# Moving the modulation sums of a two-layer backbone's up products from VectorE, ScalarE and GpSimd to TensorE

## The chip, the cores and the metric

The kernel runs on one core of one Trainium2 chip. TensorE, VectorE, ScalarE, GpSimd and SyncE are the core's engines; rows of the profile call them PE (and PEld for its weight loads), DVE, ACT, POOL and SP. The metric is the device time of one execution in microseconds (us), lower is better.

## The reference, cut to what matters

Two layers of a diffusion backbone work on 512 latent and 256 context tokens of 1024 features, all in fp32. Layer 0 mixes tokens by attention, layer 1 by a state-space layer; each is followed by a gated feed-forward with 2816 hidden features. Every sub-layer is steered by *modulations*: rows of 1024 numbers (shift, scale, gate) that come from a condition vector.

```python
silu_c = jax.nn.silu(c)          # latents' condition, 1024 numbers
silu_cc = jax.nn.silu(c_ctx)     # contexts' condition
for i in range(DEPTH):
    m_l = [... for m in jnp.split(silu_c @ w_mod[i] + b_mod[i], N_MOD, axis=-1)]
    m_c = jnp.split(silu_cc @ w_mod[i] + b_mod[i], N_MOD, axis=-1)
    ...
    h_l = modulate(rms_norm(x_lat, g_pre_ffn[i]), m_l[3], m_l[4])
    x_lat = x_lat + m_l[5] * rms_norm(conv_ffn(h_l, w_up[i], conv_w[i], conv_b[i], w_down[i]), g_post_ffn[i])
```

One modulation is a vector of 1024 times a matrix of 1024 x 1024, that is 4 MB of weights for a million multiplications: it is used once and is small work on much data. The feed-forward's first product, `h @ w_up` (768 or 512 tokens by 1024 by 5632), is the large one. It is called the up product here.

## The kernel before, in words

`ffn_up` computes the up products feature-major, in 22 *blocks* of 128 value and 128 gate features. For a block two chunks of `w_up` (128 x 1024, 512 KB) are loaded by SP into one of five slots (tag `raw`), and each is split into two fp32r parts, the rounded one by ScalarE (line 110) and the rest by VectorE (line 111). Three fp32r products then stand for one fp32 product (`mm3`, lines 147 to 149). In layer 0 each product runs over 512 latent columns (`b512`) and 256 context columns (`b256`), in layer 1 over the latents alone. The sums, two of them a block, lie in pairs of PSUM banks (tag `big`, three of them). ScalarE (872, 903) and VectorE (876 twice, 904) turn them into hidden features by the convolution and the gate; only then is the pair of banks free again.

While layer 0's up products run, two more things are done in jobs between the blocks:

- *Matrices of the state-space layer.* VectorE (1242, 1244) and GpSimd (1243) multiply tables (`PT`, later `QT`); TensorE transposes or multiplies them (`pP`, line 1261; `pK`, line 1290) into one of the two remaining PSUM banks (tag `aux`), ScalarE and VectorE take them out (1262, 1293 to 1298).
- *Later modulations.* `UP_MODS` names six units (layer, group, half): two with both conditions and three with the latents' alone in layer 0's up products, one in layer 1's. A unit takes eight chunks of `w_mod` (128 inputs x 1024 outputs, 512 KB) from the same five slots, in the same order as the chunks of `w_up`; two chunks go with a block in layer 0 from block 2 on, one with each of the blocks 8 to 15 in layer 1. `mods_ahead` (269) sums a chunk with the condition's number as a scale for each partition: for one condition VectorE alone (301) or ScalarE (295) followed by an addition on GpSimd (297). At the end of a unit TensorE adds up the partitions by a product with ones (308), and VectorE adds the bias and applies the gain (309 to 313).

Who does what next is decided when the program is built: instructions are put in order on each engine by a planner that simulates the program, and each engine then works through its own queue in that order. The order therefore shifts with any change of the code.

Of the kernel before, what the change touches and what calls it, by code (L numbers as in the profile page):

```python
# [19 lines left out]
P = 128  # L20
# [113 lines left out]
class Kernel:  # L134
# [78 lines left out]
    def mods_rows(self, l, grp):  # L213
        """The bias, and the gain of the norm that the two modulations of a group go with, as rows."""
# [17 lines left out]
    def mods_end(self, l, grp, acc, bg, psum, tag="aux", bufs=2, ms=(0, 1)):  # L232
        """Evacuates a group, stores its rows and, where they are wanted, turns them into columns."""
# [38 lines left out]
    def mods_ahead(self, psum, pool, units, lcs):  # L272
        """Modulations by other engines than the tensor engine, whose sums over partitions alone it takes; as jobs,
        one for each chunk of the weights."""
        nc, v, I = self.nc, self.nc.vector, self.I
        ones = pool.tile([P, 32], FT, name="ones")
        nc.gpsimd.memset(ones, 1.0)
        n = 64 * lcs
        for l, grp, m in units:
            b = self.small.tile([P, 512], FT, name="mbias", tag="mbias", bufs=1)[:n]  # L280
            g = self.small.tile([P, 512], FT, name="mgain", tag="mgain", bufs=1)[:n]
            name = {(0, 1): "g_pre_mix", (1, 0): "g_post_mix", (2, 0): "g_pre_ffn", (2, 1): "g_post_ffn"}.get((grp, m))
            for lc in range(lcs):
                c = slice(64 * lc, 64 * lc + 64)
                nc.sync.dma_start(b[c], dap(I["b_mod"], l * 6144 + grp * 2048 + m * D, [[512, 2], [0, 32], [1, 512]]))
                if name:
                    nc.sync.dma_start(g[c], dap(I[name], l * D, [[512, 2], [0, 32], [1, 512]]))
# [17 lines left out]
            for lc in range(lcs):  # L305
# [10 lines left out]
            for lc in range(lcs):  # L316
                nc.gpsimd.dma_start(dap(self.mdram[l, grp], lc * 2048 + m * D, [[512, 2], [1, 512]]),
                                    b[64 * lc:64 * lc + 64:32, :])
            if l and (grp, m) in ((1, 1), (2, 0)):
                p = psum.tile([P, 4, P], FT, name="pmc", tag="aux", bufs=2)  # L320
                for i in range(4):
                    nc.tensor.transpose(p[:, i, :64], b[:, i * P:(i + 1) * P], self.ident[:64, :64])
                v.tensor_copy(self.cols[1, 1][:, 0, grp - 1, :].rearrange("p (q b) -> p q b", b=4),
                              p[:, :, 0:33:32].rearrange("p b q -> p q b"))
# [35 lines left out]
    def stats(self, x, junk, tag):  # L360
        """x: rows, in one piece or in two; junk: room for their squares."""
# [14 lines left out]
    def plan_proj(self, w, nblk):  # L376
        """w: rows of inputs by columns; in blocks of 512 columns, two blocks of 128 rows a chunk."""
# [1441 lines left out]
```

## Time and profile before

| | us |
|---|---|
| median of 3 runs (lowest, highest) | 1744.71 (1743.69, 1745.6) |
| profiled execution, first to last instruction | 1744.2 |
| layer 0's up products, 421 to 922 us of it | 501 |
| layer 1's up products, 1365 to 1615 us of it | 250 |

The profile has no other time of its execution than this span; it lies 0.5 us under the median. In the rows below a busy time is the union of an engine's instructions. Matmuls are pipelined, so that each is shown longer than the step from its start to the next one's. "PEclk" is the mean clock that TensorE was granted, as a share of 2.4 GHz, its upper level; the lower one is 1.2 GHz. An engine that "waits" stands with its next instruction at the head of its queue, and all that is queued behind it waits too.

### The profile page before, as it was taken

The numbers are of one execution on the slowest core, as the hardware profiler recorded it, in microseconds if no ns is written. First come the engines' busy times: TensorE is split into PE (matmuls) and PEld (weight loads), VectorE is DVE, ScalarE is ACT, GpSimd is POOL, SyncE is SP. The second block draws the span as 40 slices with busy tenths as digits, with TensorE's granted clock in tenths as the row PEclk, the third lists the DMA queues.
The fourth block names the chain that finished last, engine by engine and source line by source line (L and its number), as shares of the span: only waits on it lengthen the run. The fifth ranks groups of instructions, "written<-read, shape, count | busy, mean of one in ns | idle before, by whom it ended". The sixth has DMA issues, their size and how long they took to land.

```text
span 1744.2 us, 22858 instructions
## 1 busy us (share of the span) xinstructions
PE 1552.6 (89%) x8376; PEld 1247.0 (71%) x8376; DVE 1166.4 (67%) x2036; ACT 772.0 (44%) x1470; POOL 373.3 (21%) x251
## 2 busy tenths in 40 slices
PE   6998489999988888998899999873789999999997
PEld 3775358888867776777788877542568888888886
DVE  4654377768999987888773357689934756565334
ACT  3564256756534333333332245555453534443322
POOL 0111060000255524334410011347501001100000
PEclk8999699999999899999999999886799999999999
DMA  9425181167354546465654269665252424432421
GB/s 308 139 73 170 37 244 47 45 225 256 116 149 136 168 135 198 126 177 179 188 144 163 97 197 273 191 170 183 91 190 85 133 85 145 134 96 97 169 73 48
DMA packets 225445, 256.39 MB, mean 147 GB/s; under 512 B 20621, under 2 KB 176917, under 8 KB 225077
## 3 DMA queue, kind: packets, MB, share of 16 engines
q1 hardware_dynamic: 224900, 254.85, 47.2%
q8 instruction: 66, 1.08, 0.3%
q14 instruction: 47, 0.38, 0.1%
q0 software_dynamic: 384, 0.07, 0.0%
q10 hardware_dynamic: 48, 0.01, 0.0%
HBM read 216.95 MB, written 34.80 MB: 144 GB/s over the span
## 4 chain that ended last, share of the span: by engine, by line
PE 58%; DVE 21%; DMA 8%; issue 5%; ACT 4%; SPq 3%; POOL 2%; DVEq 0%; ACTq 0%; POOLq 0%
PE up L147 6%; PE up L148 6%; PE up L149 6%; PE dn L148 5%; PE dn L147 5%; PE dn L149 5%; DVE whl L111 3%; PE acc L147 2%; DMA wraw<-in_w_mod 2%; PE acc L149 2%; PE acc L148 2%; DVE PT L1242 2%; PE glu L147 2%; PE glu L149 1%; PE glu L148 1%
## 5 line engine op out<-in xcount | busy, mean ns | idle before, releaser
L111 DVE TENSOR_TENSOR whl<-wraw,whl 128x1024 fp32r<-128x1024 f32 x202 | 277.0, 1376 | 176.8 <-ACT whl L110 169.0
L110 ACT ACTIVATE whl<-wraw 128x1024 fp32r<-128x1024 f32 x206 | 216.9, 1056 | 194.8 <-PE dn L149 128.2
L147 PE MATMUL up<-b,whl 128*128 128x256 f32 (+1 forms) x728 | 251.9, 349 | 23.2 <-DVE h L876 18.5
L148 PE MATMUL up<-b,whl 128*128 128x256 f32 (+1 forms) x728 | 249.9, 345 | 0.1
L149 PE MATMUL up<-b,whl 128*128 128x256 f32 (+1 forms) x728 | 249.0, 345 | 0.0
L147 PEld LDWEIGHTS up<-b,whl 128*128 128x128 f32 x728 | 144.0, 199 | 49.1 <-issue 22.6
L148 PE MATMUL dn<-whl,hs 128*128 128x512 f32 x440 | 172.9, 395 | 3.2 <-DVE whl L111 3.1
L149 PE MATMUL dn<-whl,hs 128*128 128x512 f32 x440 | 172.1, 394 | 0.0
L147 PE MATMUL dn<-whl,hs 128*128 128x512 f32 x440 | 170.7, 394 | 0.0
L148 PEld LDWEIGHTS up<-b,whl 128*128 128x128 f32 x728 | 144.4, 199 | 16.9 <-issue 2.1
L149 PEld LDWEIGHTS up<-b,whl 128*128 128x128 f32 x728 | 143.6, 198 | 15.6 <-issue 1.4
L148 PE MATMUL up<-c,whl 128*128 128x512 f32 (+1 forms) x384 | 142.5, 373 | 0.1
L149 PE MATMUL up<-c,whl 128*128 128x512 f32 (+1 forms) x384 | 141.8, 371 | 0.0
L147 PE MATMUL up<-c,whl 128*128 128x512 f32 (+1 forms) x384 | 139.4, 372 | 1.1 <-DVE c L357 1.1
L297 POOL TENSOR_TENSOR macc<-macc,wraw 128x1024 f32<-128x1024 f32 x30 | 87.9, 2930 | 201.3 <-ACT wraw L295 179.5
L876 DVE SCALAR_TENSOR_TENSOR ga<-up,cw,ga 128x511 f32<-128x511 f32 (+1 forms) x132 | 86.7, 657 | 63.9 <-ACT ga L872 62.5
L872 ACT ACTIVATE ga<-up,cw 128x512 f32<-128x512 f32 (+1 forms) x66 | 46.5, 705 | 147.3 <-PE up L149 139.5
L148 PEld LDWEIGHTS dn<-whl,hs 128*128 128x128 f32 x440 | 83.3, 189 | 22.1 <-DVE whl L111 4.1
L876 DVE SCALAR_TENSOR_TENSOR h<-up,cw,h 128x511 f32<-128x511 f32 (+1 forms) x132 | 86.6, 656 | 17.6 <-ACT h L872 16.4
L147 PEld LDWEIGHTS dn<-whl,hs 128*128 128x128 f32 x440 | 83.4, 190 | 19.2 <-ACT ga L872 0.8
L149 PEld LDWEIGHTS dn<-whl,hs 128*128 128x128 f32 x440 | 83.4, 190 | 18.2
L1243 POOL TENSOR_TENSOR QT<-tab 128x576 f32<-128x576 f32 x32 | 66.5, 2079 | 92.6 <-DVE QT L1244 54.0
(358 smaller groups left out, 3294.3 us busy)
## 6 DMA issues: line engine op xcount, KB each, us to landing
wraw<-in_w_up SPq DMA_DIRECT2D x88, 512.0 KB
wraw<-in_w_mod SPq DMA_DIRECT2D x80, 512.0 KB
wraw<-in_w_down SPq DMA_DIRECT2D x66, 512.0 KB
wraw<-in_w_o SPq DMA_DIRECT2D x24, 512.0 KB
Pt<-Pd SPq DMA_DIRECT2D x24, 512.0 KB
Pt<-Qd SPq DMA_DIRECT2D x32, 384.0 KB
wm<-in_w_mod SPq DMA_DIRECT2D x16, 512.0 KB
Pd<-Pb SPq DMA_DIRECT2D x16, 512.0 KB
```

Of the source, the lines that this page charges most:

```text
L110: nc.scalar.activation(w[:, 0], r, AF.Copy)
L111: e.tensor_tensor(w[:, 1], r, w[:, 0], op=OP.subtract)
L147: nc.tensor.matmul(out, a[0], b[0], start=start, stop=False)
L148: nc.tensor.matmul(out, a[0], b[1], start=False, stop=False)
L149: nc.tensor.matmul(out, a[1], b[0], start=False, stop=stop)
L297: nc.gpsimd.tensor_tensor(a, a, o, op=OP.add)
L872: nc.scalar.activation(o, acc, AF.Identity, scale=c[:, 1:2], bias=c[:, 3:4])
L876: nc.vector.scalar_tensor_tensor(x, acc[:, a + s:b + s], c[:, tap:tap + 1], x, op0=OP.mult, op1=OP.add)
L1242: v.tensor_tensor(t, powers(0), a, op=OP.mult)
L1243: nc.gpsimd.tensor_tensor(t2, powers(1), b, op=OP.mult)
```

## The change

`mods_ahead` no longer keeps accumulators in SBUF and no longer uses VectorE, ScalarE and GpSimd for the sums. A chunk of 128 inputs by 1024 outputs is multiplied by TensorE in plain fp32: the condition (two columns and 30 of zeros) is the stationary operand, and the four quarters of the chunk's columns go to four quarters of the partitions of one PSUM tile, 256 columns wide. It is summed there over the unit's eight chunks. The tile, `macc`, is one of the two `aux` banks and is held from a unit's first chunk to its end. Bias and gain are laid out in the same way (four loads of 32 partitions each instead of one for each condition), and two transposes of 128 columns replace four of 64.

```diff
-    def mods_ahead(self, psum, pool, units, lcs):
+    def mods_ahead(self, psum, units, lcs):
...
-            accs = [pool.tile([P, D], FT, name=f"macc{i}", tag=f"macc{i}", bufs=1) for i in range(lcs)]
+            acc = psum.tile([P, 512], FT, name="macc", tag="aux", bufs=2)[:, :256]
             for k in range(KD):
                 w = self.W.take()
-                for lc in range(lcs):
-                    a, c = accs[lc], self.cT[:, k, lc:lc + 1]
-                    if lc == lcs - 1 and (lc or k % 2):
-                        o = w if k else a
-                        nc.scalar.activation(o, w, AF.Copy, scale=c)
-                        if k:
-                            nc.gpsimd.tensor_tensor(a, a, o, op=OP.add)
-                    elif k == 0:
-                        v.tensor_scalar(a, w, c, None, op0=OP.mult)
-                    else:
-                        v.scalar_tensor_tensor(a, w, c, a, op0=OP.mult, op1=OP.add)
+                for q in range(4):
+                    nc.tensor.matmul(acc[32 * q:32 * q + 32], self.cT[:, k, :], w[:, 256 * q:256 * q + 256],
+                                     start=(k == 0), stop=(k == KD - 1))
                 if k < KD - 1:
                     yield
-            p = psum.tile([P, 512], FT, name="pm", tag="aux", bufs=2)
-            for lc in range(lcs):
-                for j in range(2):
-                    q = 64 * lc + 32 * j
-                    nc.tensor.matmul(p[q:q + 32], ones, accs[lc][:, j * 512:(j + 1) * 512], start=True, stop=True)
-            v.tensor_tensor(b, p[:n], b, op=OP.add)
+            v.tensor_tensor(b, acc, b, op=OP.add)
```

The changed file has other line numbers: line 301 of before has none, 308 is now 289 (the products with `wraw`), 309 is 293, 876 is 859, 904 is 887, 1242 is 1221, 1244 is 1223, 1261 is 1240. Three places show how the order moves.

TensorE at the end of the first unit. `up` is a block's sum, `whl` a split chunk, `pm` the sum over partitions. Before:

```order
L149 MATMUL up_5290<-b256_7_3611,whl84_5296 128x256
L308 MATMUL pm_5426<-macc0_4845,ones_4839 32x512 x2
L308 MATMUL pm_5426<-macc1_4846,ones_4839 32x512 x2
L147 MATMUL up_5497<-b512_0_3596,whl88_5503 128x512
L148 MATMUL up_5497<-b512_0_3596,whl88_5503 128x512
```

And now, where the first unit ends (86 and 87 are its last two chunks of `w_mod`):

```order
L149 MATMUL up_5294<-b512_7_3603,whl85_5304 128x512
L289 MATMUL macc_4842<-wraw86_5126,cT_70 32x256 x4
L289 MATMUL macc_4842<-wraw87_5244,cT_70 32x256
L1240 MATMUL pP_5267<-ident_60,PT_5255 128x128 x4
L289 MATMUL macc_4842<-wraw87_5244,cT_70 32x256 x3
L147 MATMUL up_5497<-b512_0_3596,whl88_5503 128x512
```

The four products of a chunk stand in TensorE's queue between two groups of up products, mostly together with those of the next chunk; at some places something else stands between a chunk's four.

TensorE at the first transposes of the state-space matrices, two tiles `pP` of one table `PT`. Before:

```order
L149 MATMUL up_4937<-b512_7_3603,whl76_4943 128x512
L1261 MATMUL pP_4905<-ident_60,PT_4899 128x128 x4
L1261 MATMUL pP_4911<-ident_60,PT_4899 128x128 x4
L147 MATMUL up_4938<-b512_0_3596,whl77_4948 128x512
```

And now (43 rows, all but a few of them up products, lie between the two pieces):

```order
L147 MATMUL up_4936<-b512_1_3597,whl76_4942 128x512
L1240 MATMUL pP_4904<-ident_60,PT_4898 128x128 x4
L149 MATMUL up_4936<-b512_1_3597,whl76_4942 128x512
...
L149 MATMUL up_4721<-b256_7_3611,whl73_4657 128x256
L1240 MATMUL pP_4910<-ident_60,PT_4898 128x128 x4
L147 MATMUL up_4937<-b512_0_3596,whl77_4947 128x512
```

While a unit runs, one `aux` bank is its own, and the two tiles of a table follow one another in the other one, at a distance, where before they stood side by side in two.

VectorE at the second table. Before:

```order
L301 SCALAR_TENSOR_TENSOR macc0_4845<-wraw86_5125,cT_70,macc0_4845 128x1024
L876 SCALAR_TENSOR_TENSOR ga_4723<-up_4721,cw_4140,ga_4723 128x255
L876 SCALAR_TENSOR_TENSOR h5120_4333<-up_4937,cw_4140,h5120_4333 128x511
L1242 TENSOR_TENSOR PT_4918<-tab_4894 128x1024
L301 SCALAR_TENSOR_TENSOR macc0_4845<-wraw87_5242,cT_70,macc0_4845 128x1024
L876 SCALAR_TENSOR_TENSOR h5120_4333<-up_4937,cw_4140,h5120_4333 128x511
```

And now:

```order
L859 SCALAR_TENSOR_TENSOR h5120_4333<-up_4936,cw_4140,h5120_4333 128x511 x2
L1221 TENSOR_TENSOR PT_4917<-tab_4893 128x1024
L859 SCALAR_TENSOR_TENSOR ga_4723<-up_4721,cw_4140,ga_4723 128x255
L111 TENSOR_TENSOR whl81_5123<-wraw81_4945,whl81_5123 128x1024
L1223 TENSOR_TENSOR PT_4917<-PT_4917,PT2_4918 128x1024
```

The sums with `wraw` are gone from between the convolution's instructions, the splits and the tables.

## Rows read from the trace of the kernel before

**Rows 1.** Busy time of each engine by stretch (count), clock, DMA share, GB/s.

```profile
520.00:620.00 100.00, 86.75 (x474) 73.44 (x473) 95.41 (x78) 40.64 (x60) 48.81 (x18) 0.91 0.54 163
820.00:920.00 100.00, 94.94 (x551) 76.87 (x552) 76.84 (x104) 32.80 (x55) 27.22 (x16) 0.95 0.53 157
880.00:920.00 40.00, 40.00 (x244) 32.40 (x243) 27.22 (x41) 14.89 (x26) 4.26 (x3) 1.00 0.39 108
421.00:922.00 501.00, 449.03 (x2669) 374.87 (x2668) 431.03 (x524) 188.52 (x303) 195.29 (x83) 0.94 0.53 157
1365.00:1615.00 250.00, 248.85 (x1196) 208.65 (x1195) 150.48 (x220) 103.92 (x139) 11.10 (x7) 1.00 0.36 111
```

The columns after the stretch and its length are PE, PEld, DVE, ACT, POOL.

**Rows 2.** Waits from 421 to 922 us: us in total, times, longest.

```profile
POOL QT L1243 <- DVE QT L1244: 54.0, 24, 6.9
ACT wraw L295 <- DMA wraw<-in_w_mod: 34.4, 8, 7.5
PE up L147 <- DVE h L876: 18.5, 12, 3.1
PE pP L1261 <- DVE PT L1244: 14.5, 8, 3.8
```

**Rows 3.** Groups of instructions from 421 to 922 us: busy, mean ns, idle before.

```profile
L111 DVE TENSOR_TENSOR whl<-wraw,whl 128x1024 fp32r<-128x1024 f32 x45 | 78.7, 1749 | 2.4 <-ACT whl L110 2.4
L297 POOL TENSOR_TENSOR macc<-macc,wraw 128x1024 f32<-128x1024 f32 x26 | 78.3, 3010 | 74.9 <-ACT wraw L295 53.1 <-DVE whl L111 7.9 <-DVE macc L299 7.4
L1242 DVE TENSOR_TENSOR QT<-tab 128x576 f32<-128x576 f32 x32 | 47.6, 1503 | 5.5 <-DMA tab<-tabd 4.7 <-PE pK L1290 0.5 <-DMA Qd<-QT 0.3
L1242 DVE TENSOR_TENSOR PT<-tab 128x1024 f32<-128x1024 f32 x16 | 41.9, 2618 | 4.6 <-PE pP L1261 4.6
L301 DVE SCALAR_TENSOR_TENSOR macc<-wraw,cT,macc 128x1024 f32<-128x1024 f32 x23 | 39.5, 1719 | 10.0 <-DMA wraw<-in_w_mod 9.9
L1244 DVE TENSOR_TENSOR QT<-QT,QT 128x576 f32<-128x576 f32 x32 | 30.1, 939 | 9.6 <-POOL QT L1243 9.5
L904 DVE TENSOR_TENSOR h<-h,ga 128x512 f32<-128x512 f32 x22 | 21.3, 969 | 5.7 <-ACT ga L903 5.7
L1262 ACT ACTIVATE Pb<-pP 128x512 f32<-128x512 f32 x32 | 17.7, 590 | 20.2 <-PE pP L1261 16.1 <-issue 4.1
L904 DVE TENSOR_TENSOR h<-h,ga 128x256 f32<-128x256 f32 x21 | 17.4, 828 | 0.3 <-ACT ga L903 0.2
L299 DVE TENSOR_SCALAR macc<-wraw,cT 128x1024 f32<-128x1024 f32 x5 | 4.5, 906 | 0.0
```

**Rows 4.** Lines over the whole span: ns min/median/max of one.

```profile
L111 DVE TENSOR_TENSOR whl<-wraw,whl x202: 1196/1225/3671, 30.9 to 1713.7; 128x1024 fp32r<-128x1024 f32 x101
...
L1242 DVE TENSOR_TENSOR QT<-tab x32: 1168/1244/2625, 677.9 to 885.7; 128x576 f32<-128x576 f32 x32
...
L1242 DVE TENSOR_TENSOR PT<-tab x16: 2008/2090/4516, 482.5 to 646.3; 128x1024 f32<-128x1024 f32 x16
...
L1244 DVE TENSOR_TENSOR QT<-QT,QT x32: 741/757/2935, 682.2 to 888.0; 128x576 f32<-128x576 f32 x32
...
L904 DVE TENSOR_TENSOR h<-h,ga x66: 408/683/3155, 445.3 to 1618.6; 128x512 f32<-128x512 f32 x44, 128x256 f32<-128x256 f32 x22
```

**Rows 5.** TensorE in order of time: start, us, what, records.

```profile
55.87 1.93 PE L540 MATMUL acc<-wm,cT 128*32 128x256 f32 x32
57.74 0.51 PE L147 MATMUL acc<-whl,a 128*128 128x512 f32 x1
...
1534.35 0.39 PE L149 MATMUL up<-c,whl 128*128 128x512 f32 x1
1534.67 1.05 PE L308 MATMUL pm<-macc,ones 128*32 128x512 f32 x4
1535.65 0.50 PE L147 MATMUL up<-c,whl 128*128 128x512 f32 x1
1535.99 0.39 PE L148 MATMUL up<-c,whl 128*128 128x512 f32 x1
1536.22 0.39 PE L149 MATMUL up<-c,whl 128*128 128x512 f32 x1
```

More of the change, by code (lines that the diff above doesn't have):

```diff
@@ L270, in mods_end @@
                         pv[:, 64 * m + lc:64 * m + lc + 33:32, :])
-    def mods_ahead(self, psum, pool, units, lcs):
+    def mods_ahead(self, psum, units, lcs):
         nc, v, I = self.nc, self.nc.vector, self.I
-        ones = pool.tile([P, 32], FT, name="ones")
-        nc.gpsimd.memset(ones, 1.0)
-        n = 64 * lcs
         for l, grp, m in units:
-            b = self.small.tile([P, 512], FT, name="mbias", tag="mbias", bufs=1)[:n]
-            g = self.small.tile([P, 512], FT, name="mgain", tag="mgain", bufs=1)[:n]
+            b = self.small.tile([P, 512], FT, name="mbias", tag="mbias", bufs=1)[:, :256]
+            g = self.small.tile([P, 512], FT, name="mgain", tag="mgain", bufs=1)[:, :256]
@@ L286, in mods_ahead @@
                 if name:
-                    nc.sync.dma_start(g[c], dap(I[name], l * D, [[512, 2], [0, 32], [1, 512]]))
-            accs = [pool.tile([P, D], FT, name=f"macc{i}", tag=f"macc{i}", bufs=1) for i in range(lcs)]
+                    nc.sync.dma_start(g[c], dap(I[name], l * D + 256 * q, [[0, 32], [1, 256]]))
+            acc = psum.tile([P, 512], FT, name="macc", tag="aux", bufs=2)[:, :256]
             for k in range(KD):
                 w = self.W.take()
-                for lc in range(lcs):
-                    a, c = accs[lc], self.cT[:, k, lc:lc + 1]
-                    if lc == lcs - 1 and (lc or k % 2):
-                        o = w if k else a
-                        nc.scalar.activation(o, w, AF.Copy, scale=c)
-                        if k:
-                            nc.gpsimd.tensor_tensor(a, a, o, op=OP.add)
-                    elif k == 0:
-                        v.tensor_scalar(a, w, c, None, op0=OP.mult)
-                    else:
-                        v.scalar_tensor_tensor(a, w, c, a, op0=OP.mult, op1=OP.add)
+                for q in range(4):
+                    nc.tensor.matmul(acc[32 * q:32 * q + 32], self.cT[:, k, :], w[:, 256 * q:256 * q + 256],
+                                     start=(k == 0), stop=(k == KD - 1))
@@ L302, in mods_ahead @@
                 if k < KD - 1:
                     yield
-            p = psum.tile([P, 512], FT, name="pm", tag="aux", bufs=2)
-            for lc in range(lcs):
-                for j in range(2):
-                    q = 64 * lc + 32 * j
-                    nc.tensor.matmul(p[q:q + 32], ones, accs[lc][:, j * 512:(j + 1) * 512], start=True, stop=True)
-            v.tensor_tensor(b, p[:n], b, op=OP.add)
+            v.tensor_tensor(b, acc, b, op=OP.add)
             if (grp, m) in ((0, 1), (2, 0)):
@@ L316, in mods_ahead @@
             for lc in range(lcs):
-                nc.gpsimd.dma_start(dap(self.mdram[l, grp], lc * 2048 + m * D, [[512, 2], [1, 512]]),
-                                    b[64 * lc:64 * lc + 64:32, :])
+                nc.gpsimd.dma_start(dap(self.mdram[l, grp], lc * 2048 + m * D, [[256, 4], [1, 256]]), b[lc:P:32, :])
             if l and (grp, m) in ((1, 1), (2, 0)):
[L320 to L324, printed above, removed]
+                p = psum.tile([P, 2, P], FT, name="pmc", tag="aux", bufs=2)
+                for i in range(2):
+                    nc.tensor.transpose(p[:, i], b[:, i * P:(i + 1) * P], self.ident)
+                v.tensor_copy(self.cols[1, 1][:, 0, grp - 1, :].rearrange("p (q b) -> p q b", b=2),
+                              p[:, :, 0:P:32].rearrange("p b q -> p q b"))
             yield
@@ L995, in mods @@
             for i, units in enumerate(UP_MODS[0]):
-                mp = self.pool(f"mods{i}", "right")
-                for j, _ in enumerate(self.mods_ahead(ps, mp, units, 2 - i)):
-                    if j == KD * len(units) - 1:
-                        mp.release()
-                    yield
+                yield from self.mods_ahead(ps, units, 2 - i)
         def rows_of(pool, lc):
@@ L1744, in ffn1 @@
         self.bits = True
-        def mods():
-            mp = self.pool("mods2", "right")
-            for j, _ in enumerate(self.mods_ahead(ps, mp, UP_MODS[1][0], 1)):
-                if j == KD - 1:
-                    mp.release()
-                yield
-        self.ffn_up(1, ((self.act, LAT),), "right", lambda: iter(()), [0] * NF, mods())
+        self.ffn_up(1, ((self.act, LAT),), "right", lambda: iter(()), [0] * NF, self.mods_ahead(ps, UP_MODS[1][0], 1))
         self.actp.release()
```

4 lines of the change are left out of this document (2 added, 2 removed).

## The prediction

> **What bounds the kernel now.** I read the two stretches with up products by engine first, since the change touches nothing else. In layer 1's ([rows 1], its last row) TensorE is busy for 248.85 of 250 us at full clock (1.00) and VectorE for 150: TensorE is the bound there, and whatever is added to it is paid. In layer 0's ([rows 1], the fourth row) it is less clear: TensorE is busy for 449 of 501 us, VectorE for 431. The waits [rows 2] show which of the two is late. TensorE stands 18.5 us before up products because VectorE has not yet read the sums out of the PSUM banks that they need (line 876), and 14.5 us before `pP` because the table is not ready (1244). So VectorE holds TensorE up. Its idle time has a second price, the clock: over the 501 us the granted clock is 0.94, that is some 12% of the stretch at 1.2 GHz, which costs up to 0.06 x 501 = 30 us of TensorE's progress. TensorE's own work at 2.4 GHz is then 501 - 52 (idle) - 30 (clock) = 419 us, and 82 us are overhead.
>
> How this overhead goes with VectorE's load is seen by reading the same view in three pieces, the first three of [rows 1]. From 520 to 620 VectorE is 95.4% busy; TensorE idles 13.3 us and loses 9 by its clock (0.91): 22%. From 820 to 920 VectorE is 76.8% busy, and it is 5.1 + 5 = 10%. From 880 to 920 it is 27.2 of 40 us, 68%, and TensorE loses nothing.
>
> **What TensorE gets.** The price of a chunk isn't in this trace as such, but its shape is: line 540 multiplies 256 columns by 32 stationary ones into four quarters of the partitions, and 308 does it with 512 columns into two. One fp32 product is two records. In the first two of [rows 5] 32 records, sixteen products or four rounds over the quarters, take 57.74 - 55.87 = 1.87 us until the next product starts, 0.47 a round at most. The products in different quarters thus run at the same time. The last four rows bound what it costs to enter and leave such a round amid up products: from line 149's start at 1534.35 to 148's at 1535.99 are 1.64 us, of which two steps are the up products' own (0.23 each, as from 1535.99 to 1536.22). That leaves 1.18 us for a round of 512 columns. Calling a round of 256 columns a, and entry and exit together e: 2a + e = 1.18, and 4a plus something between nothing and e is 1.87, so a lies between 0.35 and 0.47 and e between 0.49 and 0.25. I take a = 0.43, e = 0.32. By the order of the changed kernel the 40 chunks of layer 0 stand in 28 places; where other work cuts a chunk's four products apart, a round counts twice, so that there are 48 rounds: 48 x 0.43 + 28 x 0.32 = 29.6 us, and 29.3 to 30.3 with the two ends. In layer 1 the eight chunks stand in 12 places of one round each: 12 x 0.75 = 9.0 us (8.6 to 10.1). What goes are the sums over partitions, line 308: five in layer 0 and one in layer 1, 1.18 each, 5.9 and 1.2 us. The transposes at a unit's end are too few to count. Net, TensorE gets 23.7 us in layer 0 and 7.8 in layer 1.
>
> **What VectorE loses.** Line 301 and 299 go: 39.5 + 4.5 = 44 us in layer 0 [rows 3]. More goes indirectly. VectorE's instructions with two SBUF operands are drawn out while GpSimd works. [Rows 3] give their mean here and [rows 4] what one takes undisturbed: 45 x (1749 - 1196) ns for line 111, 32 x (1503 - 1168) and 16 x (2618 - 2008) for 1242, 32 x (939 - 741) for 1244, 21 x (828 - 408) for 904 on 256 columns and 22 x (969 - 683) on 512, together 24.9 + 10.7 + 9.8 + 6.3 + 8.8 + 6.3 = 66.8 us. GpSimd is busy for 195 us of the stretch, 78.3 of them with line 297, which goes: 40%, so 27 us of it. I take it all the same in proportion, since the rest, line 1243, is as long an instruction and works against the same ones. The bounds are nothing (the tables' own products just move into the gap) and 66.8. VectorE is left with 431 - 44 - 27 = 360 us. ScalarE loses line 295; it was busy for 188.5 of 501 us and hides it. The bias and gain loads grow from one or two to four a row of numbers; they are small and are needed only at the end of a unit, some 80 us after they are issued, but they stand in SP's queue ahead of weights.
>
> The Trainium skill (SBUF — State Buffer, "Who interferes with whom") calls the read port that VectorE and GpSimd share an exclusive lock: whoever comes second stands until the other's whole instruction is over. The maximum of 3671 ns for line 111 against 1196 fits one such full wait, but its mean of 1749 shows that most instructions don't meet one. If all 26 additions of 3.0 us held VectorE up for their full length, the relief would be 44 + 78 us, VectorE would fall to 309, and the stretch would come near 452 us, the case of a larger gain below. The mean is the measurement, and the sum stays with it.
>
> **The sum.** TensorE's own work in layer 0 becomes 419 + 23.7 = 443 us. With T the new length, VectorE is busy for 360/T. For T = 481 that is 75%; between the pieces at 68% (nothing lost) and at 76.8% (10%) this reads as 8%, and 443/0.92 = 481. So layer 0's stretch shrinks by 20 us and layer 1's grows by 8: 1744.2 - 20 + 8 = 1732 us for the profiled execution, and the same for the median, which lies 0.5 above it. The ends: with 2% lost, T = 452 and the time is 1703; with the full 82 us of overhead kept, T = 525 and the time is 1776.
>
> **What is queued behind the new waits.** A modulation's product waits at the head of TensorE's queue for its chunk, and all up products wait behind it. Before, it was ScalarE that stood there: 34.4 us in 8 waits [rows 2]. In the order the load of nearly every chunk is released tens of up products before its use, more than 10 us; only four, three in the first unit and one in the third, have some 25 to 45 products in between, 4 to 8 us, which is about what the longest of those waits was (7.5). I count nothing for it, and a few us belong to the range.
>
> **The rivals.**
>
> *One bank for the tables (slower).* While a unit runs, `macc` keeps one of two `aux` banks, so the 64 tiles `pP` and `pK` pass through one, each only after the one before has been taken out. ScalarE needs 0.59 us for a `pP` ([rows 3], line 1262) once it comes to it. For it: the pairs of before stood side by side in TensorE's queue, and if ScalarE or VectorE are late, TensorE now stands. Against it: the planner has put mostly 10 to 45 up products (2 to 10 us) between two tiles. If each costs 0.5 us more, that is 32 us: 1764. It decides from 12/64 = 0.2 us a tile on. The Trainium skill (Perfetto Trace Analysis, "Optimizing Tensor Performance") says that independent groups of matmuls should rotate through different banks, so that taking one out overlaps the next; by it this rival would be the rule. No row of before shows one bank alone.
>
> *TensorE inherits the waits for weights (slower).* If the 34.4 us pass to it whole: 1766. Against it: those loads were late because their slots were held by sums that ScalarE and GpSimd took one after another, and TensorE frees a slot by one round.
>
> *The tables set the pace.* GpSimd waits 54 us for VectorE's part of `QT` [rows 2], and VectorE for GpSimd's in turn; if this chain decides the stretch, layer 0 stays at 501 us and only layer 1's 8 are left: 1752.
>
> *A larger gain.* If VectorE at 75% holds TensorE up no more than at 68%, overhead falls to 2% or less: 1694 to 1703.
>
> **How the numbers follow.** The forecast, 1718 to 1741, gets 0.42; a gain short of it, within 0.2% (3.5 us, about what a measurement of this kernel can tell from no change), 0.10; the larger gain 0.16; one bank 0.13, inherited waits 0.08, the tables 0.11. So faster 0.58, same 0.10, slower 0.32. The range, 1702 to 1762, leaves out some of the largest gain and the upper ends of the first two rivals.
>
> **What would show it.** Right: in layer 0's stretch VectorE's mean for line 111 falls towards 1.4 us, its busy time to about 360, TensorE's clock rises above 0.96 and its waits for line 876 shrink; the new products, line 289, step by 0.43 us a round; layer 1's stretch is 8 us longer with TensorE still full. Wrong: waits of `pP` or `pK` on lines 1262 or 1293 to 1298 (one bank), waits of line 289 on `in_w_mod` (inherited), or the stretch unchanged while TensorE idles on tables.

## The result and the profile after

The changed kernel takes 1726.81 us (median of 4 runs, 1722.4 to 1734.74) beside 1745.15 us for the kernel before on the same chip: a ratio of 0.9897, 95% interval 0.9871 to 0.9923: about 1% faster, clear of the noise. The profiled execution spans 1723.3 us, 20.9 less than the one of before.

First the two stretches with up products, by engine (stretch, length, then PE, PEld, DVE, ACT, POOL busy, clock, DMA share, GB/s). They answer to the last two of [rows 1]; layer 0's now begins at 423.6 and ends at 884.0, layer 1's runs from 1336.1 to 1594.0.

```profile
424.00:884.00 460.00, 437.57 (x2936) 360.02 (x2934) 351.99 (x495) 159.91 (x275) 108.57 (x55) 0.99 0.57 169
1336.10:1594.00 257.90, 256.75 (x1254) 209.42 (x1255) 143.93 (x215) 99.97 (x133) 1.32 (x2) 1.00 0.36 107
```

Layer 0's stretch is 41 us shorter, VectorE's busy time in it has fallen from 431 to 352 us, TensorE stands for 22 us instead of 52, and its clock is 0.99 instead of 0.94. Layer 1's is 8.2 us longer, and TensorE is still full there.

Part of the 41 us is only a border. The last block's down products (`dn`) begin before layer 0's last up product, and how many of them lie ahead of it depends on the order. The same view for `dn` alone, of the kernel before:

```profile
421.50:922.80 501.30, 7.32 (x31) 5.74 (x31) 0.00 (x0) 0.00 (x0) 0.94 0.53 157
```

and of the changed kernel:

```profile
423.60:884.00 460.40, 2.19 (x9) 1.52 (x9) 0.00 (x0) 0.00 (x0) 0.99 0.57 169
```

Before, 31 records of down products were done inside the stretch, now 9. Without them layer 0's up products took 501.3 - 7.3 = 494.0 us before and take 460.4 - 2.2 = 458.2 now: 35.8 us less. (The down products can be taken out by their busy time because TensorE has no gaps there: [rows 1], 880 to 920 us.) The 5.1 us of down products come behind the stretch instead. This net length is used below.

The difference of the two executions is then: +2.1 us ahead of the stretch (it starts at 423.6, not 421.5), -35.8 in it, +8.2 in layer 1's, and +4.6 elsewhere, together -20.9. Most of the 4.6 lies in the state-space layer's outputs, where TensorE waits longer for ScalarE. From the waits of 884 to 1336 us of the changed kernel (us in total, times, longest):

```profile
PE py L1584 <- ACT SA L1569: 22.9, 4, 11.2
```

and of 923 to 1365 us of the kernel before:

```profile
PE py L1605 <- ACT SA L1590: 11.5, 3, 7.0
```

The waits in layer 0's stretch, which answer to [rows 2] (us in total, times, longest; `Ks`, lines 1273 and 1277, read `pK` out of its bank):

```profile
ACT whl L110 <- DMA wraw<-in_w_up: 40.6, 12, 7.2
...
PE pK L1269 <- DVE QT L1223: 5.3, 4, 2.1
...
PE pK L1269 <- DVE Ks L1273: 4.3, 2, 3.7
...
PE pK L1269 <- DVE Ks L1277: 3.4, 2, 3.0
...
PE pP L1240 <- DVE PT L1223: 3.0, 1, 3.0
...
PE up L147 <- DVE ga L859: 1.9, 3, 0.9
```

Of the kernel before, beside [rows 2]:

```profile
PE up L147 <- DVE ga L876: 4.6, 4, 2.8
PE pK L1290 <- DVE Ks L1298: 4.0, 1, 4.0
```

TensorE's waits for VectorE before up products fell from 18.5 + 4.6 = 23.1 to 1.9 us, that before `pP` from 14.5 to 3.0. The waits before `pK` did not fall; most of what TensorE still stands idle is there. ScalarE no longer stands before chunks of `w_mod`; it now stands 40.6 us before chunks of `w_up`, and no wait of TensorE for it is in the view.

The groups of instructions from 421 to 884 us that answer to [rows 3] (busy, mean ns, idle before):

```profile
L111 DVE TENSOR_TENSOR whl<-wraw,whl 128x1024 fp32r<-128x1024 f32 x45 | 74.7, 1661 | 24.0 <-ACT whl L110 24.0
...
L1221 DVE TENSOR_TENSOR QT<-tab 128x576 f32<-128x576 f32 x32 | 47.9, 1507 | 5.4 <-DMA tab<-tabd 4.0 <-DMA Qd<-QT 1.1 <-issue 0.3
...
L1221 DVE TENSOR_TENSOR PT<-tab 128x1024 f32<-128x1024 f32 x16 | 34.5, 2156 | 9.1 <-PE pP L1240 4.6 <-DMA tab<-tabd 4.4
...
L1223 DVE TENSOR_TENSOR QT<-QT,QT 128x576 f32<-128x576 f32 x32 | 24.1, 752 | 7.0 <-POOL QT L1222 6.7
...
L887 DVE TENSOR_TENSOR h<-h,ga 128x512 f32<-128x512 f32 x22 | 19.1, 866 | 10.2 <-ACT ga L886 10.1
...
L887 DVE TENSOR_TENSOR h<-h,ga 128x256 f32<-128x256 f32 x21 | 10.9, 521 | 1.6 <-ACT ga L886 1.6
L289 PEld LDWEIGHTS macc<-wraw,cT 128*32 128x32 f32 x320 | 9.8, 110 | 11.3 <-issue 6.0 <-DVE Ks L1277 0.8 <-DMA wraw<-in_w_mod 0.4
```

The relief of VectorE is uneven: the tables `PT` fell from 2618 to 2156 ns, 904 (now 887) on 256 columns from 828 to 521, but the splits (line 111) only from 1749 to 1661 and the tables `QT` not at all (1503 and 1507). The last row shows that the new products waited 0.4 us for their chunks.

What one place of them costs is seen in layer 1, TensorE in order of time (start, us, what, records):

```profile
1459.06 0.39 PE L149 MATMUL up<-c,whl 128*128 128x512 f32 x1
1459.38 0.63 PE L289 MATMUL macc<-wraw,cT 128*32 128x256 f32 x6
1459.94 0.50 PE L147 MATMUL up<-c,whl 128*128 128x512 f32 x1
1460.28 0.39 PE L148 MATMUL up<-c,whl 128*128 128x512 f32 x1
```

From line 149's start to 148's are 1.22 us; two steps of 0.23 are the up products' own, so a place of one round costs 0.76 us (six of a round's eight records are in the trace here).

### The profile page after: what moved, and what is told of

Its sections match the earlier page's. It is cut to its first block, busy times and chain, and to the rows that moved or that the text cites. A ratio compares the mean times of both kernels' runs of the same rounds, so it can differ in the third digit from the quotient of the medians.

```text
span 1723.3 us, 23398 instructions
## 1 busy us (share of the span) xinstructions
PE 1552.6 (90%) x8724; PEld 1236.6 (72%) x8724; DVE 1082.5 (63%) x2004; ACT 740.8 (43%) x1438; POOL 274.8 (16%) x218
## 4 chain that ended last, share of the span: by engine, by line
PE 63%; DVE 16%; DMA 9%; issue 4%; ACT 4%; SPq 3%; POOL 1%; DVEq 0%; ACTq 0%; POOLq 0%
PE up L147 8%; PE up L148 8%; PE up L149 8%; PE dn L147 5%; PE dn L148 5%; PE dn L149 5%; DVE whl L111 2%; DMA wraw<-in_w_up 2%; PE acc L147 2%; PE acc L149 2%; PE acc L148 2%; PE glu L147 2%; PE glu L149 2%; PE glu L148 2%; DVE QT L1221 1%
## 5 line engine op out<-in xcount | busy, mean ns | idle before, releaser
L111 DVE TENSOR_TENSOR whl<-wraw,whl 128x1024 fp32r<-128x1024 f32 x202 | 270.5, 1344 | 202.3 <-ACT whl L110 201.1
L147 PE MATMUL up<-b,whl 128*128 128x256 f32 (+1 forms) x728 | 244.2, 338 | 1.9 <-DVE ga L859 1.9
L148 PE MATMUL up<-b,whl 128*128 128x256 f32 (+1 forms) x728 | 242.3, 335 | 0.0
L149 PE MATMUL up<-b,whl 128*128 128x256 f32 (+1 forms) x728 | 241.7, 335 | 0.0
L147 PEld LDWEIGHTS up<-b,whl 128*128 128x128 f32 x728 | 137.3, 189 | 25.6 <-issue 9.2
L148 PEld LDWEIGHTS up<-b,whl 128*128 128x128 f32 x728 | 137.6, 189 | 16.4 <-issue 2.0
L149 PEld LDWEIGHTS up<-b,whl 128*128 128x128 f32 x728 | 136.8, 189 | 15.0 <-issue 1.5
L855 ACT ACTIVATE ga<-up,cw 128x512 f32<-128x512 f32 x66 | 46.5, 705 | 150.1 <-PE up L149 148.4
L859 DVE SCALAR_TENSOR_TENSOR h<-up,cw,h 128x511 f32<-128x511 f32 (+1 forms) x132 | 86.7, 657 | 37.2 <-ACT h L855 35.8
L148 PEld LDWEIGHTS dn<-whl,hs 128*128 128x128 f32 x440 | 83.3, 190 | 22.9 <-DVE whl L111 4.9
L149 PEld LDWEIGHTS dn<-whl,hs 128*128 128x128 f32 x440 | 83.2, 189 | 18.3
L1222 POOL TENSOR_TENSOR PT<-tab 128x1024 f32<-128x1024 f32 x16 | 44.5, 2783 | 321.5 <-DMA tab<-tabd 254.3
L886 ACT ACTIVATE ga<-ga 128x512 f32<-128x512 f32 x66 | 36.9, 560 | 114.6 <-DVE ga L859 110.7
```

Source lines behind the costliest of these rows:

```text
L111: e.tensor_tensor(w[:, 1], r, w[:, 0], op=OP.subtract)
L147: nc.tensor.matmul(out, a[0], b[0], start=start, stop=False)
L148: nc.tensor.matmul(out, a[0], b[1], start=False, stop=False)
L149: nc.tensor.matmul(out, a[1], b[0], start=False, stop=stop)
L855: nc.scalar.activation(o, acc, AF.Identity, scale=c[:, 1:2], bias=c[:, 3:4])
L859: nc.vector.scalar_tensor_tensor(x, acc[:, a + s:b + s], c[:, tap:tap + 1], x, op0=OP.mult, op1=OP.add)
```

## The experiments

One table for all, from the windows over the stretch of layer 0's up products ("net" is without the down products in it, "tables in pieces" the number of pieces in which the transposes `pP` stand among the up products in TensorE's order). Each of e1 to e10 was run once. Three groups ran on one chip each; the kernel before took 1743.23 us beside the first four, 1745.75 beside the next four and 1746.74 (median of 9) beside the last four.

| kernel | us | stretch | net | VectorE busy | clock | tables in pieces |
|---|---|---|---|---|---|---|
| before (its profile) | 1744.71 | 501.3 | 494.0 | 431 | 0.94 | 18 |
| changed (its profile) | 1726.81 | 460.4 | 458.2 | 352 | 0.99 | 25 |
| e1, before without GpSimd's additions | 1725.89 | 472.1 | 469.5 | 389 | 0.96 | 17 |
| e2, before without VectorE's sums | 1737.72 | 486.0 | 483.1 | 401 | 0.96 | 18 |
| e3, before without either | 1730.47 | 480.7 | 478.2 | 367 | 0.96 | 18 |
| e4, the program of before once more (see there) | 1740.62 | 496.3 | 489.0 | 429 | 0.96 | 18 |
| e5, before, chunks read by nobody | 1733.97 | 478.3 | 475.7 | 364 | 0.95 | 19 |
| e6, before without ScalarE's scaling | 1760.59 | 506.1 | 498.8 | 422 | 0.95 | 18 |
| e7, changed, ScalarE reads too | 1729.62 | 462.1 | 460.2 | 351 | 0.99 | 25 |
| e8, changed, VectorE sums too | 1745.56 | 483.4 | 481.5 | 389 | 0.99 | 24 |
| e9, changed, thin products | 1722.30 | 467.6 | 458.0 | 350 | 0.97 | 26 |
| e10, changed, products twice | 1754.66 | 484.3 | 484.3 | 358 | 0.99 | 26 |
| e11, changed in layer 0 alone | 1714.86 | 463.2 | 461.0 | 353 | 0.98 | 25 |
| e12, changed again | 1726.02 | 459.0 | 456.8 | 352 | 0.99 | 25 |

The rows of the kernel before and of e4 come from the same program and differ by 5 us in the stretch; the changed kernel's two by 1.4. Differences of a few us between two single runs therefore show nothing.

**e1: GpSimd's additions alone.** The kernel before without line 297.

```diff
                         nc.scalar.activation(o, w, AF.Copy, scale=c)
-                        if k:
-                            nc.gpsimd.tensor_tensor(a, a, o, op=OP.add)
```

> The kernel before with GpSimd's 30 additions (line 297) left out, so that the modulations lack these terms; VectorE's own sums, ScalarE's scaling and the order of the loads stay. Layer 0's up products took 501 us in the kernel before. If VectorE's whole load holds TensorE up, GpSimd's additions are worth the 27 us by which they drew VectorE's other instructions out: VectorE falls from 431 to about 404 us busy and the stretch to 480 to 490 us, the whole to about 1727 to 1734. If the port that GpSimd and VectorE share is the whole story, the stretch falls to about 455 us or less. If neither counts (only the slots' release or the tables do), it stays within 5 us of 501.

The stretch in the windows view:

```profile
424.30:896.40 472.10, 432.94 (x2648) 360.55 (x2647) 388.79 (x523) 187.77 (x302) 117.99 (x57) 0.96 0.57 165
```

VectorE does what it did, but is busy for 42 us less: that is what 78 us of additions on GpSimd had cost it. The net stretch is 24.5 us shorter, more than was expected. GpSimd's own queue is relieved too, and with it its part of the tables, so this run alone doesn't tell the two apart.

**e2: VectorE's sums alone.** The kernel before without line 301.

```diff
-                    else:
-                        v.scalar_tensor_tensor(a, w, c, a, op0=OP.mult, op1=OP.add)
```

> The kernel before with VectorE's 26 sums of line 301 left out, so that the modulations lack these terms; GpSimd's additions stay. If VectorE's whole load holds TensorE up, it falls by about 40 us of its own to about 390, and layer 0's stretch to 470 to 485 us, the whole to about 1714 to 1730. If only the shared port counts, the stretch stays within 5 us of 501.

The net stretch is 10.9 us shorter and the total 1737.72 us, less of a gain than expected. VectorE's busy time falls by 30 us, not by the 39.5 of the sums, since GpSimd's additions stay and VectorE's other instructions meet them: the splits took 1851 ns on average, 1749 before, and the tables `QT` 1689, 1503 before.

**e3: neither.** Both edits at once.

> The kernel before with both left out, lines 297 and 301: the modulations are wrong, the weights are still loaded. TensorE gets no new products here. If the relief of VectorE is what the change brings and the new products are what it costs, the stretch is shorter than the changed kernel's 460 us by about their 19 to 24 us: 435 to 442, and layer 1's stays at 249; the whole is 1744 - 62 = 1682, within 8. If the two relieve the same waits, it is less than the sum of the two runs with one left out. If the tables set the pace, the stretch stays at 455 us or above.

This contradicts the theory that VectorE's load alone sets the stretch: VectorE is down to 367 us, but the net length is 478.2 us, longer than in e1. ScalarE stood 82.2 us before chunks of `w_mod` in it (34.4 before). I took that wait for a second cause; e5 to e7 try it. The stretch in the windows view, and two of VectorE's waits (421 to 905 us):

```profile
424.80:905.50 480.70, 431.54 (x2647) 360.11 (x2646) 367.15 (x500) 187.58 (x302) 115.71 (x57) 0.96 0.55 162
```

```profile
DVE PT L1238 <- DMA tab<-tabd: 15.7, 4, 7.5
DVE QT L1238 <- DMA tab<-tabd: 12.0, 4, 3.8
```

VectorE stands 27.7 us before tables that have not come from memory (4.7 before), so here too leaving the sums out brought a new wait.

**e4: the bank, an edit without effect.** The kernel before, but `pm` is declared at the start of a unit, as `macc` is, and was meant to take its `aux` bank there.

```diff
+            p = psum.tile([P, 512], FT, name="pm", tag="aux", bufs=2)
             accs = [pool.tile([P, D], FT, name=f"macc{i}", tag=f"macc{i}", bufs=1) for i in range(lcs)]
...
-            p = psum.tile([P, 512], FT, name="pm", tag="aux", bufs=2)
```

> The kernel before, complete, with one edit: the PSUM tile for the sum over partitions is taken at a unit's start, not at its end, so that one of the two aux banks is held as long as the changed kernel holds it. If one bank for the tables costs time, layer 0's stretch is longer than 501 us, by 0.2 to 0.5 us for each of 64 tiles, 13 to 32 us. If it is hidden, it stays within 4 us.

1740.62 beside 1743.23 us. But the edit changed nothing in the program: every engine has the same instructions with the same addresses in the same order as before, since `pm` is still written at the unit's end alone and gets its bank only there. The trace of e4 shows it inside the first unit:

```profile
508.93 1.07 PE L1261 MATMUL pP<-ident,PT 128*128 128x128 f32 x8 [0.41 <-DVE PT L1244]
```

Eight records in 1.07 us are two tiles one right behind the other, and ScalarE needs 0.59 us to take one out: both banks were free for tables. What one bank costs, e4 doesn't say. What it does give is the spread of one program over two executions: 501.3 and 496.3 us of stretch.

**e5: read by nobody.**

```diff
                     a, c = accs[lc], self.cT[:, k, lc:lc + 1]
-                    if lc == lcs - 1 and (lc or k % 2):
...
-                    elif k == 0:
+                    if k == 0:
                         v.tensor_scalar(a, w, c, None, op0=OP.mult)
-                    else:
-                        v.scalar_tensor_tensor(a, w, c, a, op0=OP.mult, op1=OP.add)
```

> The kernel before, in which nothing reads the modulation chunks any more, except that VectorE scales the first of each unit; ScalarE's scaling, VectorE's sums and GpSimd's additions are left out (so the modulations are those of one chunk). Revised theory (what cost layer 0's up products was VectorE's load and also ScalarE standing at the head of its queue until a chunk of the modulations' weights had come): with both gone and no new products on TensorE, the stretch of layer 0's up products, 501 us before, 472 to 486 in the first three experiments and 460 in the changed kernel, takes 435 to 445 us, and layer 1's 249 to 251. Rival A (the tables' pace or the planner's order sets the stretch, whoever reads the chunks): 465 to 485. Rival B (VectorE's load alone): like the experiment without both sums, about 480.

The net stretch is 475.7 us, not 435 to 445: with ScalarE's wait gone nothing is gained over e3. But this kernel has a wait of its own. SyncE's longest waits from 424 to 903 us:

```profile
SPq L815 <- DMA wraw<-in_w_mod: 58.8, 17, 7.9
...
SPq L206 <- DMA wraw<-in_w_mod: 36.8, 10, 5.8
```

Where no engine reads a chunk, the next load into its slot waits on SP for the chunk itself to land, 95.6 us in all, and the tables' loads stand behind it in the same queue. VectorE's groups (421 to 905 us) show it:

```profile
L1234 DVE TENSOR_TENSOR QT<-tab 128x576 f32<-128x576 f32 x32 | 50.6, 1592 | 24.8 <-DMA tab<-tabd 13.5 <-DMA Qd<-QT 11.3
...
L1234 DVE TENSOR_TENSOR PT<-tab 128x1024 f32<-128x1024 f32 x16 | 34.5, 2159 | 18.7 <-DMA tab<-tabd 15.7 <-PE pP L1253 2.9
```

It waits 29.2 us for tables from memory, 8.4 in the changed kernel. A kernel that leaves the reading out is thus no clean case of "the change without its products".

**e6: without ScalarE's scaling.** GpSimd adds the chunk as it came.

```diff
-                        nc.scalar.activation(o, w, AF.Copy, scale=c)
-                        if k:
+                        if k == 0:
+                            nc.scalar.activation(o, w, AF.Copy, scale=c)
+                        else:
                             nc.gpsimd.tensor_tensor(a, a, o, op=OP.add)
```

> The kernel before without ScalarE's scaling of the chunks behind the first of a unit: GpSimd adds the chunk as it came (so the sums are not weighted), and VectorE and GpSimd do what they did. Revised theory (ScalarE's wait for the chunks at the head of its queue costs TensorE): layer 0's stretch falls from 501 to 480 to 491 us though VectorE's and GpSimd's work is untouched, and TensorE's waits for VectorE's gate products and convolution, 18.5 us before, shrink by half. Rival (ScalarE's wait is covered by other work): 497 to 505 us.

The stretch is not shorter but 5 us longer, which is the spread of one program, and the total is 15 us longer.

**e7: ScalarE back.** The changed kernel with the scaling of before beside the products.

```diff
                                      start=(k == 0), stop=(k == KD - 1))
+                if lcs > 1 or k % 2:
+                    nc.scalar.activation(old[0], w, AF.Copy, scale=self.cT[:, k, 0:1])
```

> The changed kernel, in which ScalarE, as before the change, also scales the chunks (all of layer 0's first two units, every second one of the other units), into a tile that nobody reads. Revised theory: layer 0's stretch, 460 us in the changed kernel, grows to 470 to 485 us by ScalarE's waits for the chunks, though VectorE does nothing more. Rival (ScalarE's wait is covered): 457 to 464 us.

460.2 us net against 458.2, although ScalarE stands 60.4 us before these chunks, as its group (421 to 905 us) shows:

```profile
L293 ACT ACTIVATE old<-wraw,cT 128x1024 f32<-128x1024 f32 x28 | 32.3, 1152 | 61.5 <-DMA wraw<-in_w_mod 60.4 <-issue 1.1
```

With e6 this ends the theory of ScalarE's wait: other work covers it.

**e8: VectorE back.** The changed kernel with VectorE's sums of before beside the products, into a tile that nobody reads.

```diff
+                if lcs > 1 or k % 2 == 0:
+                    if k == 0:
+                        v.tensor_scalar(old[0], w, self.cT[:, k, 0:1], None, op0=OP.mult)
+                    else:
+                        v.scalar_tensor_tensor(old[0], w, self.cT[:, k, 0:1], old[0], op0=OP.mult, op1=OP.add)
```

> The changed kernel, in which VectorE, as before the change, also sums chunks (one sum for each chunk of layer 0's first two units, every second chunk of the other units), into a tile that nobody reads. Theory of the prediction (VectorE's load is what paces the stretch): its some 38 sums of 1.2 us are 45 us more on VectorE, which then has about 398 us of work in the stretch, and the stretch grows from 460 to 475 to 490 us. Rival (TensorE itself is the bound by now and VectorE has the room): 460 to 466 us.

```profile
423.20:906.60 483.40, 445.40 (x2937) 361.57 (x2935) 389.02 (x523) 159.47 (x274) 112.28 (x55) 0.99 0.54 161
```

The sums are 28 in the stretch, not the 38 of the expectation. 37 us more on VectorE make the net stretch 23.3 us longer, and in the total the whole gain of the change is gone: 1745.56 beside 1745.75 us. (In the stretch 12.5 of the 35.8 us are left.) TensorE's products are the same, and its order is nearly so, with the tables in 24 pieces instead of 25. But VectorE doesn't only work more, it also stands before the chunks. From its waits (421 to 905 us):

```profile
DVE old L296 <- DMA wraw<-in_w_mod: 14.1, 10, 2.9
...
DVE old L294 <- DMA wraw<-in_w_mod: 4.2, 1, 4.2
```

These 18.3 us (9.9 in the kernel before) belong to what e8 puts into VectorE's queue; which share of the 23.3 is theirs was not separated.

**e9: thin products.** Every product behind a unit's first chunk takes 32 columns of each quarter and starts its sum anew; the order stays nearly that of the changed kernel.

```diff
+                n = 32 if k else 256
                 for q in range(4):
-                    nc.tensor.matmul(acc[32 * q:32 * q + 32], self.cT[:, k, :], w[:, 256 * q:256 * q + 256],
-                                     start=(k == 0), stop=(k == KD - 1))
+                    nc.tensor.matmul(acc[32 * q:32 * q + 32, :n], self.cT[:, k, :], w[:, 256 * q:256 * q + n],
+                                     start=True, stop=True)
```

> The changed kernel with TensorE's products of every chunk behind the first of a unit cut from 256 columns in each quarter to 32 (so the modulations are those of parts of the sums). In the order of TensorE's instructions the tables' products stay where the changed kernel has them, in 26 pieces up to block 11.5 and from block 12.6 on, where the kernels without new products have them in 17 to 19 pieces up to block 10.3 to 10.9 and from 11.5 to 12.0 on. Theory now (the new products brought another order, in which the tables' products stand finer and later among the up products, and that is why the changed kernel's layer 0 is shorter than VectorE's relief accounts for): layer 0's stretch is 445 to 462 us, no longer than the changed kernel's 460, with TensorE's granted clock at 0.98 or more. Rival (the new products themselves fill TensorE's waits and hold its clock): without their work the stretch goes to 470 to 485 us, as in the experiments without sums or without readers.

The windows view:

```profile
422.40:890.00 467.60, 439.02 (x2969) 368.34 (x2969) 350.36 (x496) 160.70 (x274) 107.96 (x55) 0.97 0.57 169
```

And the same for `dn` alone:

```profile
422.40:890.00 467.60, 9.60 (x40) 7.47 (x41) 0.00 (x0) 0.00 (x0) 0.97 0.57 169
```

The raw 467.6 us lie between the two expectations. They hold 40 records of down products, 9.6 us; net it is 458.0 us, the changed kernel's 458.2. The clock, 0.97, is lower than the theory asked for. This run has later tables too. From VectorE's waits (421 to 905 us):

```profile
DVE PT L1222 <- PE pP L1241: 13.9, 5, 4.2
...
DVE PT L1222 <- DMA tab<-tabd: 9.9, 2, 7.5
DVE QT L1222 <- DMA tab<-tabd: 7.6, 4, 2.3
```

It stands 17.5 us for tables from memory and 13.9 for `pP`, where the changed kernel has 8.4 and 4.6.

**e10: products twice.** Each round of four products stands twice.

```diff
-                for q in range(4):
-                    nc.tensor.matmul(acc[32 * q:32 * q + 32], self.cT[:, k, :], w[:, 256 * q:256 * q + 256],
-                                     start=(k == 0), stop=(k == KD - 1))
+                for r in range(2):
+                    for q in range(4):
+                        nc.tensor.matmul(acc[32 * q:32 * q + 32], self.cT[:, k, :], w[:, 256 * q:256 * q + 256],
+                                         start=(k + r == 0), stop=(k + r == KD))
```

> The changed kernel with each new product done twice, one behind the other (the modulations come out doubled): 0.43 us more a chunk, 17 us in layer 0's stretch and 3.4 us in layer 1's, no new places. If TensorE is by now the bound in layer 0, the stretch goes from 460 to 472 to 480 us; if VectorE still paces it and TensorE has the room, 458 to 467. Layer 1's stretch, where TensorE is full: from 257.9 to 261 to 262 us.

```profile
421.60:905.90 484.30, 465.17 (x3244) 369.70 (x3245) 357.83 (x493) 162.05 (x275) 108.03 (x54) 0.99 0.54 160
```

The stretch, which has no down products in it, is 26.1 us longer net. That is more than 17: the planner put the products in 50 places instead of 31 (counted in the traces; the prediction counted 28 in the order), which at 0.32 us for entry and exit are another 6, and in 18 instead of 12 in layer 1 (264.5 us there). A second round at the same place costs what was expected; TensorE in layer 1:

```profile
1483.73 0.39 PE L149 MATMUL up<-c,whl 128*128 128x512 f32 x1
1484.05 1.07 PE L290 MATMUL macc<-wraw,cT 128*32 128x256 f32 x16
1485.05 0.50 PE L147 MATMUL up<-c,whl 128*128 128x512 f32 x1
1485.39 0.40 PE L148 MATMUL up<-c,whl 128*128 128x512 f32 x1
```

1.66 us from 149 to 148, less 0.46 for the up products' steps, is 1.20 for two rounds: 0.44 us more than the 0.76 for one.

**e11: layer 0 alone.** Layer 1's unit goes back to VectorE, ScalarE and GpSimd, with the loop of before under the name `mods_aside`.

```diff
-        self.ffn_up(1, ((self.act, LAT),), "right", lambda: iter(()), [0] * NF, self.mods_ahead(ps, UP_MODS[1][0], 1))
+        def mods():
+            mp = self.pool("mods2", "right")
+            for j, _ in enumerate(self.mods_aside(ps, mp, UP_MODS[1][0], 1)):
...
+        self.ffn_up(1, ((self.act, LAT),), "right", lambda: iter(()), [0] * NF, mods())
```

> The changed kernel, but layer 1's unit of modulations is summed by VectorE, ScalarE and GpSimd as before the change. Layer 1's stretch of up products takes 249.7 us in place of 257.9 and layer 0's is the changed kernel's 458 to 464: about 8 us less than the changed kernel on the same chip, 1717 to 1720 us, ratio to the kernel before 0.984 to 0.987. Rival (the stages behind layer 1's products take the 8 us back, or its order shifts): within 3 us of the changed kernel.

**e12: the changed kernel again**, beside e11.

> The changed kernel as it is, for the comparison on the same chip: 1722 to 1735 us, ratio 0.987 to 0.992, layer 0's stretch 458 to 464 us and layer 1's 257.9.

e11 takes 1714.86 us (5 runs, 1710.53 to 1719.79), a ratio of 0.9813 to the kernel before (0.9796 to 0.983); e12 takes 1726.02 us (4 runs, 1722.42 to 1728.5), 0.9882 (0.9864 to 0.99). The intervals don't meet. Both stretches of e11:

```profile
423.40:886.60 463.20, 442.77 (x2938) 364.12 (x2936) 352.82 (x495) 161.08 (x275) 109.09 (x55) 0.98 0.57 168
1338.90:1588.60 249.70, 248.56 (x1195) 208.66 (x1195) 150.03 (x219) 103.44 (x138) 11.10 (x7) 1.00 0.37 110
```

Layer 1's products are back at 249.7 us: where TensorE is full, VectorE, ScalarE and GpSimd do the sums for nothing. Of the 11 us between the two medians this explains 8.2; the profile of e11 is that of its slowest run, so where the other 3 lie can't be read from it.

## Why the prediction was right, and where it was not

**Layer 1: right.** 12 places at 0.75 us, less the sum over partitions, made 7.8 us; the trace has 8.2, the place costs 0.76, and e11 gets the 8.2 back by undoing this part alone.

**What TensorE gets in layer 0: right, somewhat high.** From the windows, TensorE's busy time less the clock's loss and the down products was 449.0 - 0.06 x 501 - 7.3 = 412 us before and is 437.6 - 0.01 x 460 - 2.2 = 431 now: 19 us more, where the sum had 23.7. The prediction's 419 us had 7 us of down products in them.

**What VectorE loses: right, somewhat low.** 431 - 352 = 79 us, of which 44 are the sums and 35 the rest, in the main relief from GpSimd, where the sum had 27. The choice of the mean over one full wait for each addition came nearer: the Trainium skill (SBUF — State Buffer, "Who interferes with whom") describes an exclusive lock, by which 78 us of additions could have cost VectorE up to 78; the runs show 35 here and 42 in e1. That line 111 would fall towards 1.4 us was wrong, it is 1.66.

**The overhead: the step that failed.** "For T = 481 that is 75%; between the pieces ... this reads as 8%, and 443/0.92 = 481." VectorE is indeed at 352/460 = 76.5%, but TensorE idles 22 us and loses some 4 by its clock: 26 us or 5.7% of the stretch, where the sum had 481 - 443 = 38. T is 460. Of the 21 us between, 12 are this overhead, 5 are the down products that moved out of the stretch and are done later, and the rest is the work of TensorE that was put too high.

Not only the size is off. The sum read the overhead from VectorE's share of the stretch, and the runs show that this share doesn't set it. At 75 to 77% in all three, idle time and the clock's loss are 26 us in the changed kernel, 28.6 + 0.03 x 468 = 43 in e9 (9%) and 49.2 + 0.04 x 481 = 68 in e3 (14%).

The sum also put all of TensorE's new work on top. In e9 TensorE has 439.0 - 0.03 x 468 - 9.6 = 415 us of its own, 16 less than the changed kernel, and the stretch is as long: more idle time and a lower clock take up the difference. In e10 it has 465.2 - 0.01 x 484 = 460, 29 more, and the stretch grows by 26, although TensorE stands idle for 19 us there. So taking 16 us of columns away made the stretch no shorter, and adding 29 us made it 26 longer, in one run each. Entering and leaving the places, some 10 us at 0.32, is in e9 as in the changed kernel; whether that is free too, no run shows. Why e9 is not shorter is not shown either: VectorE's pace, its later tables and its lower clock are all there at once.

**What TensorE waits for: VectorE's queue, for a good part.** e8 shows it: the same products on TensorE, VectorE's sums put back, and 23.3 of the 35.8 us are lost. e1, from the other side, has VectorE 42 us less busy and is 24.5 us shorter. Both make it about 0.6 us of the stretch for one of VectorE, but e8 has the waits for chunks in it and e1 the relief of GpSimd; e2 (30 us less, 10.9 us shorter) makes it 0.4. At 0.6, 79 us would be worth 46 to 50, and 35.8 came; the difference can be the price of the new products or a price that falls with VectorE's load.

VectorE's load is not all. e3 and e5 have VectorE at 367 and 364 us and no new products, and need 478 and 476 us net, 18 to 20 more than e9 at 350. Two things differ there: tables that come late from memory (27.7 and 29.2 us of VectorE's waits, 17.5 in e9), and the order, in which the tables' transposes stand in 18 and 19 pieces where they have 24 to 26 with the new products. What either is worth was not separated and stays open.

**Not in the sum:** 2.1 us ahead of the stretch and 4.6 behind it. Most of the latter goes with the wait for `SA` (22.9 us, 11.5 before; 24.4 in e12's profile), in work that the change doesn't touch. In e6, which has no new products, it is 24.0 us, so they are not its cause. I take it for the order but tried nothing on it. The 2.1 us say nothing: e4, the program of before, starts its stretch 2.7 us later.

So the forecast of 1732 us against 1726.8 holds two errors of opposite sign: layer 0 gave 35.8 net where 20 were forecast, and 6.7 us elsewhere were not foreseen. That it lies within 6 us of the median is in part luck.

**The rivals.** One bank for the tables: no experiment tests it, since e4 changed nothing. The changed kernel's own waits give a measure. TensorE stands 4.3 + 3.4 = 7.7 us before `pK` until VectorE has taken the tile before out, 4.0 in the kernel before, and never before `pP` for ScalarE: some 4 us more, not 32. What the bank did to the planner's order is not in that. The Trainium skill's rule that independent groups should rotate through banks (Perfetto Trace Analysis, "Optimizing Tensor Performance") has little to gain here by these waits, with the tiles standing apart in TensorE's order. Inherited waits for weights: 0.4 us, not 34.4. The tables' pace at an unchanged 501 us: no. The larger gain came nearest in its stretch (452 us, measured 460), but its condition didn't come: overhead is 5.7%, not 2% or less.

## What to carry to other kernels

Moving work between engines pays where the engine that loses it holds the other one up, and costs its full price where the engine that gets it has no gaps: the same edit gained 36 us in layer 0 and lost 8 in layer 1, and the fastest kernel of these runs makes it in layer 0 alone. Don't take overhead as a share that one engine's load sets, with new work added on top; three kernels with VectorE at 75 to 77% had 26, 43 and 68 us of it. Before two stretches are compared, look at what the order has moved across their borders (here 5 us of down products), and before a read is left out in an experiment, ask whose wait it ends. And before an edit is believed to be a test, look in the order or the trace whether it changed anything (e4 didn't).

## What the runs showed of the hardware

- Removing 78 us of GpSimd's additions made VectorE's unchanged work 42 us shorter (e1): about half of the time of these additions had been lost on VectorE.
- Four fp32 products of 256 columns into four quarters of the partitions pass in 0.44 us together (layer 1 of e10), and one place amid other products costs 0.32 us to enter and leave.
- Less work on TensorE came with a lower clock: e9, with 16 us less to do in the same 458 us, stood idle for 29 us instead of 22 and was granted 0.97 of its upper level where the changed kernel had 0.99 (e11, with the same layer 0, 0.98).
- A load into a slot whose last content nobody reads waits for the earlier load to land (e5: 95.6 us on SP), and all other loads of that queue wait with it.
